# First adaLN pair in two channel halves, splits two units ahead and late loads in sixteen slots, before a 32-expert MoE

## The chip, the cores and the metric

The kernel runs on one NeuronCore of one Trainium2 chip. The metric is the device time of one execution in microseconds. TensorE is PE in the rows, VectorE DVE, ScalarE ACT, GpSimd POOL and SyncE SP; the queue of an engine that issues DMAs has a q behind its name (SPq).

## The reference, cut to what matters

256 tokens of width 1024 go through one layer; everything is float32.

```python
ada = (silu(c) @ w_ada + b_ada)                       # w_ada 1024 x 6144
sh_m, sc_m, g_m, sh_f, sc_f, g_f = split(ada, 6)
h = rms_norm(x, norm_mix_g) * (1 + sc_m) + sh_m
proj = h @ w_in                                       # w_in 1024 x 4000
q_lat, kv_lat, k_pe, u, c_gate, b_gate, g_attn, g_conv = split(proj)
a_branch = attention(q_lat, kv_lat, k_pe; w_uq, w_ukv) @ w_up_attn
c_branch = (b_gate * causal_conv3(c_gate * u)) @ w_up_conv
x = x + g_m * ((sigmoid(g_attn) * a_branch + sigmoid(g_conv) * c_branch) @ w_o)
h = rms_norm(x, norm_ffn_g) * (1 + sc_f) + sh_f
# top-4 of 32 experts; expert e: gu = h @ w_gu[e] + b_gu[e]; y = swiglu(gu) @ w_down[e] + b_down[e]
x = x + g_f * moe(h);  out = rms_norm(x) * g_final
```

The weights of the mixer are some 48 MB, those of the experts (w_gu 1024 x 2048 and w_down 1024 x 1024 for each of 32) some 403 MB. All are read once.

## The kernel before

**Two stages.** The front (adaLN, projections, attention, convolution, gates, w_o, router) takes the first 244 us of the profile; then the 32 experts follow, each for up to 64 tokens gathered by one-hot matmuls. Every engine works through its own instructions in the order in which the code emits them; nothing is reordered, so an instruction that waits holds up all behind it on that engine. The DMA queue of SP is such an order too: nearly all loads go through it.

**Slots.** All weights pass through one SBUF pool. In the front it is 22 "narrow" slots of 8 KB for each partition, and the MoE stage sees the same memory as 11 "wide" slots of 16 KB, wide slot i being narrow slots 2i and 2i+1. `take` hands out the free slot that has been free longest, `give` returns one, and `pump` issues the next loads of the list `loads` while more than `spare` slots are free. In the front `spare` is 9. Once the list is empty, `take` prefers a slot whose neighbour in the wide pair is free.

**Projections.** Weights come in "units" of [128, 4, 416 or 512] or [128, 2, 1024] (1 MB), k = 0 to 25, in the order in which they are used. `split` (lines 342 to 349) turns a raw unit into a high part (ACT copy, L346) and a low part (DVE subtraction, L347); each product is three matmuls (L335 to L337, or L477 in `proj`): high by high, high by low, low by high. The table `LOOK` sets for each unit how many later units are split by then.

**adaLN.** The first pair (shift_m, scale_m) needs all rows of w_ada by 2048 columns: eight chunks of 1 MB, 128 rows of 8 KB each (L120), then 32 matmuls of 512 columns (L251). The sums are transposed to columns (L320) and give `sh_col` and `a_col` (L330 to L332); with these the normalised x, transposed on PE (L302), becomes the high part of h (ACT, L417), a float32 copy (DVE, L420) and the low part (DVE, L423). The second pair (gate_m, shift_f) is multiplied on PE, the third (scale_f, gate_f) is accumulated on DVE chunk by chunk (L446) and summed over partitions by `ada_sum` on PE (L453), between the two halves of the attention branch.

**The end of the front.** After gate 3: the halves of the attention output (ACT L689, POOL L690), the attention branch with w_up_attn in two parts k = 0 and 1, `merge_t(0)` (transposes L797), `wo_mm(0, ...)`, `merge_t(1)`, `wo_mm(1, ...)` and the router. `bias_load` (L855) loads b_gu into a narrow slot by four DMAs on SP's queue, just after the last w_o unit and just ahead of the first expert weights (L999). `bias_table` (L863) works on it later, on ACT and POOL.

**The experts.** Each needs four w_gu loads and two w_down loads of 2 MB; each fills a wide slot as soon as both its narrow slots, or the load before in that slot, are done with.

Of the kernel before, what the change touches and what calls it, by code (L numbers as in the profile page):

```python
# [16 lines left out]
P = 128  # L17
D = 1024
# [33 lines left out]
def ap_of(a, offset, dims):  # L52
    return bass.AP(tensor=a.tensor, offset=a.offset + offset, ap=dims)
# [3 lines left out]
def block_kernel(ctx, tc, x, c, positions, w_ada, b_ada, norm_mix_g, w_in, q_norm_g, w_uq, kv_norm_g,  # L57
# [16 lines left out]
    class Slots:  # L74
        def __init__(self, pool, since, size):
            self.pool, self.since, self.held, self.clock, self.spare = pool, since, {}, max(since), 0

            for i in range(len(since)):
                pool.tile([P, size], F32, name="w", tag=f"w{i}", bufs=1)

        def take(self, shape, dtype=F32):

            i = min((not loads and self.since[(i ^ 1) % len(self.since)] is not None, c, i)
                    for i, c in enumerate(self.since) if c is not None)[2]
            self.since[i] = None
# [25 lines left out]
    def mmt():  # L111
        return mm.tile([P, 512], F32, name="mm")
# [4 lines left out]

    def ada0_chunk(j):
        w = slot([2048])
        load(w, ap_of(w_ada, j * 6 * D, [[8 * 6 * D, P], [1, 2048]]))  # L120
        return w
# [72 lines left out]
    with tc.tile_pool(name="front", bufs=1) as fr, \  # L194
# [29 lines left out]
        def rows_in(dst, src):  # L224
            return lambda: load(dst, src)
# [5 lines left out]
                 rows_in(pvec[18:19], kv_norm_g),  # L231
                 rows_in(pvec[19:31], conv_w.rearrange("o k (q p) -> (o k q) p", p=P))]
        small += [rows_in(brow[g][32 * b:32 * b + 1, :], b_ada[:, (4 * g + b) * 512:(4 * g + b + 1) * 512])
                  for g in range(3) for b in range(4)]
        ada0 = []
        for j in range(8):
            ada0.append(ada0_chunk(j))
            if j:
                for f in small[3 * j - 3:3 * j]:
                    f()  # L240

# [11 lines left out]

        def ada0_mm(j):
            ada_mm(pa, j, ada0[j])
            give(ada0[j])

# [9 lines left out]
        V.tensor_scalar(xn[:, 1, :], xs[:, 1, :], r0[:, 1:2], None, op0=ALU.mult)  # L267
        for j in range(2):
            ada0_mm(j)
        pos_f = ft("pos_f", [NT, P], 2, "pe1")  # L270
# [22 lines left out]

        for j in range(2, 6):
            ada0_mm(j)
        xps = []
        for q2 in range(4):
            p = (mmt() if q2 == 3 else tpt()).rearrange("p (q t) -> p q t", t=T)
            xps.append(p)
            for q in range(2):  # L300
                for i in range(NT):
                    TE.transpose(p[:, q, i * P:(i + 1) * P],  # L302
                                 xn[:, i, (2 * q2 + q) * P:(2 * q2 + q + 1) * P], ident)
        give(xn)
        for j in range(6, 8):
            ada0_mm(j)
        ppc = mmt()
# [18 lines left out]
        arow = slot([512])  # L326
        V.tensor_add(arow, brow[0], pa)
        pcv = halves_t(arow, mmt(), lambda q: slice(q * P, (q + 1) * P))
        give(arow)
        V.tensor_copy(by_half(sh_col[:, 0, :]), pcv[:, 0:2, :, 0])  # L330
        V.tensor_scalar(by_half(a_col[:, 0, :]), pcv[:, 2:4, :, 0], 1.0, None, op0=ALU.add)
        V.tensor_mul(a_col[:, 0, :], a_col[:, 0, :], gmix)  # L332

# [8 lines left out]

        def split(raw, shape):
            hi = slot(shape, F32R)
            lo = slot(shape, F32R)
            S.activation(hi, raw, AF.Copy)  # L346
            V.tensor_tensor(lo, raw, hi, op=ALU.subtract)  # L347
            give(raw)
            return [hi, lo]
# [6 lines left out]

        jobs = [win_unit(0, 416, h) for h in range(2)]
        jobs += [win_unit(928, 512, h) for h in range(2)]
        jobs += [([2, 768], w_uq.rearrange("o (q p) f -> p (o q) f", p=P)),
# [27 lines left out]
        units, chunks = [raw_load(*j) for j in jobs], [ada_load(*j) for j in ada_todo]  # L387
        loads += [(chunks if c == "a" else units).pop(0) for c in "wwwwwwwwwaaawwawwwwaaaawwwaawaawwwawawaaww"]
        narrow.spare = 9

        def ahead(n):
            while len(done) < min(n, len(jobs)):
                need(lambda: len(raws) > len(done))
                done.append(split(*raws[len(done)]))


        LOOK = [2, 2, 4, 3, 4, 1, 2, 0, 2, 0, 4, 1, 1, 0, 2, 2, 2, 1, 3, 3, 3, 0, 0, 0, 0, 0]

# [10 lines left out]


        ahead(1)
        hT = [slot([NQ, T], F32R), slot([NQ, T], F32R)]
        h32 = slot([NQ, T])
        for half in range(2):
# [9 lines left out]
            ahead(half + 2)  # L424
        give(h32)
        S.dma_start(rw.rearrange("p (a b) e -> p a b e", b=2), router_w.rearrange("o (a p b) e -> p (o a) b e", p=P, b=2))
# [55 lines left out]

        def projT(u, ps, half):
            for m in range(4):
                for q in range(4):
# [11 lines left out]

        pl = two()
        u = unit()
        proj(u, pl, 0, 416)  # L500
        proj(unit(), pl, 1, 416)
# [24 lines left out]

        pc_ = twoT()
        projT(unit(), pc_, 0)
        projT(unit(), pc_, 1)

# [856 lines left out]
```

## Time and profile before

| | |
|---|---|
| median of three runs | 1178.86 us (1177.23 to 1180.64) |
| the profiled execution, its own time | 1177.89 us |
| its span | 1176.2 us |
| mean granted clock of TensorE | 0.971 of full |
| PE busy | 1073.2 us, 91% |
| DVE, ACT, POOL busy | 360.1, 152.0 and 36.7 us |
| read from HBM | 455.79 MB, 388 GB/s over the span |

The page cuts the span into 40 slices of 29.4 us. Its line "DMA" gives the busy share of the 16 DMA engines in tenths, "GB/s" what they moved. A busy PE is not PE at its peak. The DMA line has to be read by stage: the mean over the span hides that the first eight slices are uneven and the rest are flat. The window view gives the same for any stretch, with the granted clock (PEclk). The wait view says for each line how long an engine or queue stood, and on whom. The timeline gives start and duration; what is in square brackets is the idle time just before, and what ended it.

### The profile page before, as it was taken

Reading aid. Unit: us, or ns where it says so; the run is one execution under the profiler, and the core shown is the slowest. Engines: PE = TensorE matmul, PEld = TensorE weight load, DVE = VectorE, ACT = ScalarE, POOL = GpSimd, SP = SyncE. Lnnn points to the kernel's source line nnn. Section 1 sums busy time; section 2 is a strip of 40 time slices with the busy share of each in tenths; the row PEclk is TensorE's granted clock in tenths of the full one; section 3 lists DMA queues with packets and bytes.
Section 4 is the critical chain, followed back from the end, with each engine's and each line's share of the span. In section 5 each row is a group of like instructions: output and inputs, shape, how many; then the busy total and the mean of one; then the engine's idle time right before and its main releaser. Section 6 shows DMA issues by size and latency. Waiting matters only on the chain. (4 is left out here: it accounts for less than half of the span.)

```text
span 1176.2 us, 11805 instructions
## 1 busy us (share of the span) xinstructions
PE 1073.2 (91%) x4914; PEld 492.1 (42%) x4914; DVE 360.1 (31%) x703; ACT 152.0 (13%) x261; POOL 36.7 (3%) x85
## 2 busy tenths in 40 slices
PE   5898997999999999999999879999888988898996
PEld 1887775753343343323433234334223422342333
DVE  3857588423221222111212112131212121211123
ACT  1545642211000010000000000000000000000001
POOL 1000003100000000000000000000000000000000
PEclk9899998979999999998999989999999999998998
DMA  9983853899999999999999999999999999999995
GB/s 362 354 286 116 316 210 146 359 428 428 428 428 428 428 426 417 427 429 427 428 427 428 427 426 428 427 427 427 428 427 427 428 427 427 427 428 428 427 420 180
DMA packets 48206, 457.66 MB, mean 389 GB/s; under 512 B 4939, under 2 KB 10088, under 8 KB 20756
## 3 DMA queue, kind: packets, MB, share of 16 engines
q1 hardware_dynamic: 47394, 456.58, 93.1%
q8 instruction: 41, 0.67, 0.2%
q10 hardware_dynamic: 674, 0.14, 0.1%
q0 software_dynamic: 80, 0.14, 0.0%
q14 instruction: 17, 0.14, 0.0%
HBM read 455.79 MB, written 1.05 MB: 388 GB/s over the span
## 5 line engine op out<-in xcount | busy, mean ns | idle before, releaser
L1072 PE MATMUL pg<-w,hsel 128*64 128x512 f32 x2048 | 458.6, 601 | 28.1 <-DMA w<-in_w_gu 28.0
L1072 PEld LDWEIGHTS pg<-w,hsel 128*64 128x64 f32 x2048 | 142.9, 138 | 328.1 <-issue 273.8
L1110 PE MATMUL pm<-w,aT 128*64 128x512 f32 (+1 forms) x1056 | 227.8, 582 | 12.1 <-DMA w<-in_w_down 10.5
L1090 DVE TENSOR_SCALAR ga<-pg 128x512 f32<-128x512 f32 x32 | 22.1, 691 | 463.3 <-PE pg L1072 447.1
L1110 PEld LDWEIGHTS pm<-w,aT 128*64 128x64 f32 x1056 | 74.3, 137 | 160.8 <-issue 133.3
L1091 ACT ACTIVATE sgm<-ga 128x512 f32<-128x512 f32 x32 | 20.2, 630 | 689.4 <-DVE ga L1090 689.4
L1116 DVE TENSOR_TENSOR yp<-gfx,pm 64x512 f32<-64x512 f32 x62 | 42.5, 685 | 199.9 <-PE pm L1110 199.4
L1044 PE MATMUL pm<-oh,xs 128*128 128x256 f32 (+1 forms) x256 | 58.6, 389 | 5.0 <-DVE oh L1031 5.0
L477 PE MATMUL mm<-w 128*128 128x512 f32 (+1 forms) x240 | 58.5, 404 | 3.0 <-ACT w L417 3.0
L347 DVE TENSOR_TENSOR w<-w 128x2048 fp32r<-128x2048 f32 (+3 forms) x26 | 57.2, 2235 | 8.3 <-ACT w L346 8.1
L1044 PEld LDWEIGHTS pm<-oh,xs 128*128 128x128 f32 x256 | 50.5, 204 | 16.6 <-issue 11.5
L335 PE MATMUL mm<-w 128*128 128x256 f32 (+1 forms) x160 | 54.9, 343 | 1.7 <-ACT w L689 1.2
L1135 PE MATMUL mm<-yp,s 128*128 128x512 f32 x120 | 54.9, 600 | 0.8 <-DVE yp L1116 0.8
L337 PE MATMUL mm<-w 128*128 128x256 f32 (+1 forms) x160 | 53.5, 334 | 2.1 <-POOL w L690 2.0
L336 PE MATMUL mm<-w 128*128 128x256 f32 (+1 forms) x160 | 53.2, 332 | 0.0
L477 PEld LDWEIGHTS mm<-w 128*128 128x128 f32 x240 | 47.8, 200 | 11.8 <-ACT w L417 3.9
L346 ACT ACTIVATE w<-w 128x2048 fp32r<-128x2048 f32 (+3 forms) x26 | 46.3, 1838 | 11.9 <-DMA w<-in_w_in 11.9
L335 PEld LDWEIGHTS mm<-w 128*128 128x128 f32 x160 | 31.0, 194 | 8.9 <-issue 3.9
L1135 PEld LDWEIGHTS mm<-yp,s 128*128 128x128 f32 x120 | 22.1, 190 | 29.9 <-issue 27.5
L1221 POOL CAST sel<-id 128x256 fp32r<-128x256 f32 x32 | 12.7, 402 | 684.0 <-PE pg L1224 683.9
L337 PEld LDWEIGHTS mm<-w 128*128 128x128 f32 x160 | 31.1, 194 | 6.2 <-POOL w L690 2.4
L251 PE MATMUL pa<-w,cact 128*32 128x512 f32 x128 | 22.1, 775 | 12.5 <-DVE rs_v L142 8.4
(282 smaller groups left out, 626.5 us busy)
## 6 DMA issues: line engine op xcount, KB each, us to landing
w<-in_w_gu SPq DMA_DIRECT2D x128, 2048.0 KB, 39.1
w<-in_w_down SPq DMA_DIRECT2D x62, 2048.0 KB, 39.1
w<-in_w_ada SPq DMA_DIRECT2D x24, 1024.0 KB, 5.8
w<-in_w_in SPq DMA_DIRECT2D x14, 1024.0 KB, 9.4
w<-in_w_o SPq DMA_DIRECT2D x4, 1024.0 KB, 7.0
w<-in_w_up_conv SPq DMA_DIRECT2D x2, 1024.0 KB
w<-in_w_up_attn SPq DMA_DIRECT2D x2, 1024.0 KB, 7.2
w<-in_w_down SPq DMA_DIRECT2D x4, 512.0 KB, 32.3
```

What stands on the lines that cost most here:

```text
L251: TE.matmul(pa[32 * b:32 * b + 32, :], cact[:, j:j + 1].to_broadcast([P, 32]), w[:, b * 512:(b + 1) * 512], start=(j == 0), stop=(j == 7), ...
L335: TE.matmul(o, l[0], r[0], start=start, stop=False, skip_group_check=True)
L336: TE.matmul(o, l[0], r[1], start=False, stop=False, skip_group_check=True)
L337: TE.matmul(o, l[1], r[0], start=False, stop=stop, skip_group_check=True)
L346: S.activation(hi, raw, AF.Copy)
L347: V.tensor_tensor(lo, raw, hi, op=ALU.subtract)
L477: TE.matmul(ps[i][:, :n], hT[l][:, 4 * half + q, i * P:(i + 1) * P], u[r][:, q, :], start=(half == 0 and q == 0 and l == 0 and r == 0), st ...
L1044: TE.matmul(p[:, q, :], xs[:, i, fcols(2 * q2 + q)], oh[:, i, :n], start=(i == 0), stop=(i == NT - 1))
L1072: TE.matmul(pg[64 * g:64 * g + 64, n, :], hs[k // 4][:, k % 4, c0:c0 + CAP], w[:, f0:f0 + 512], start=False, stop=(k == NQ - 1), skip_grou ...
L1110: TE.matmul(py[64 * h:64 * h + 64, :], aT[:, qa, 64 * g:64 * g + 64], w[:, h], start=(b == 0), stop=(b == 7), skip_group_check=True)
L1116: V.tensor_mul(yp[64 * k2:64 * k2 + 64, h * 512:(h + 1) * 512], gfx[hp, :], py[hp, :])
L1135: TE.matmul(acc[i][h], s2[:n, i * P:(i + 1) * P], yp[:n, h * 512:(h + 1) * 512], start=start, stop=False, skip_group_check=True)
```

## The change

1. **adaLN's first pair in two channel halves.** The 2048 columns are loaded as two halves of 512 shift and 512 scale columns. A chunk is now [128, 2, 2, 512], loaded by two DMAs of 512 KB with rows of 2 KB: four chunks for channels 0 to 511, four for channels 512 to 1023. The matmuls have 256 columns, 64 instead of 32. Each half has its own sum, transposes and columns (`cols0`) and its own `h_half`. The transposes of x come before them; the last two PSUM tiles are copied to SBUF (`xT1`). The first four units change order: both 416- and 512-column units of half 0, then those of half 1, and the loads are put between the chunks to match. `projT` of unit 1 has the last two chunks of half 1 between its column blocks.
2. **Low parts behind h.** For the first units the DVE subtraction of a split is kept back until `h_half` has been emitted.
3. **Splits and slots.** `LOOK` is nearly everywhere 2; `loads` alternates units and adaLN chunks; `spare` starts at 8 and falls to 4; from unit 10 on `take` uses only the first sixteen slots as long as one of them is free.
4. **b_gu** is loaded by POOL's queue.

```diff
@@ class Slots
+            self.upto = len(since)
         def take(self, shape, dtype=F32):
-
-            i = min((not loads and self.since[(i ^ 1) % len(self.since)] is not None, c, i)
-                    for i, c in enumerate(self.since) if c is not None)[2]
+            i = min((i >= self.upto, c, i) for i, c in enumerate(self.since) if c is not None)[2]
@@ adaLN
-    def ada0_chunk(j):
-        w = slot([2048])
-        load(w, ap_of(w_ada, j * 6 * D, [[8 * 6 * D, P], [1, 2048]]))
+    def ada0_chunk(hb, j2):
+
+        w = slot([2, 2, 512])
+        for k in range(2):
+            load(w[:, k], ap_of(w_ada, (2 * j2 + k) * 6 * D + 512 * hb, [[8 * 6 * D, P], [D, 2], [1, 512]]))
         return w
...
+        def cols0(hb, p):
+
+            cs = slice(256 * hb, 256 * hb + 256)
+            V.tensor_add(arow[:, cs], brow[0][:, cs], pa[:, cs])
+            for q in range(2):
+                TE.transpose(p[:, q * P:(q + 1) * P], arow[:, 256 * hb + q * P:256 * hb + (q + 1) * P], ident)
...
-        def split(raw, shape):
+        def split(raw, shape, later=None):
             hi = slot(shape, F32R)
             lo = slot(shape, F32R)
+
+            def low():
+                V.tensor_tensor(lo, raw, hi, op=ALU.subtract)
+                give(raw)
+
             S.activation(hi, raw, AF.Copy)
-            V.tensor_tensor(lo, raw, hi, op=ALU.subtract)
-            give(raw)
+            if later is None:
+                low()
+            else:
+                later.append(low)
             return [hi, lo]
...
-        jobs = [win_unit(0, 416, h) for h in range(2)]
-        jobs += [win_unit(928, 512, h) for h in range(2)]
+        jobs = [win_unit(c0, n, h) for h in range(2) for c0, n in ((0, 416), (928, 512))]
...
-        LOOK = [2, 2, 4, 3, 4, 1, 2, 0, 2, 0, 4, 1, 1, 0, 2, 2, 2, 1, 3, 3, 3, 0, 0, 0, 0, 0]
+        LOOK = [2, 1, 2, 3, 2, 2, 2, 2, 2, 2, 2, 2, 2, 2, 2, 2, 2, 2, 2, 2, 2, 0, 0, 0, 0, 0]
 
         def unit():
             k = taken[0]
             taken[0] += 1
+            narrow.spare = {4: 7, 8: 6, 14: 5, 18: 4}.get(k, narrow.spare)
+            if k == 10:
+                narrow.upto = 16
...
         pl = two()
-        u = unit()
-        proj(u, pl, 0, 416)
+        pc_ = twoT()
+        proj(unit(), pl, 0, 416)
+        ada0_mm(1, 0)
+        ada0_mm(1, 1)
+        projT(unit(), pc_, 0, (lambda: None, lambda: ada0_mm(1, 2), lambda: ada0_mm(1, 3), lambda: cols0(1, tpt())))
+        h_half(1)
+        lows.pop()()
+        give(arow, xT1, h32)
         proj(unit(), pl, 1, 416)
...
-                    load(raw[64 * k:64 * k + 64, t, :], rows[64 * t:64 * t + 64, :])
+                    G.dma_start(raw[64 * k:64 * k + 64, t, :], rows[64 * t:64 * t + 64, :])
```

How the order of instructions moves. **SP's queue at the end of the front**, before (w is a slot, xN a run of N equal rows):

```order
L375 DMA w<-in_w_ada 128x2048 x2
L382 DMA w<-in_w_o 128x2x1024 x2
L855 DMA w<-in_b_gu 64x512 x4
L999 DMA w<-in_w_gu 128x4096 x8
L999 DMA w<-in_w_down 128x4096 x2
```

and after:

```order
L402 DMA w<-in_w_o 128x2x1024
L395 DMA w<-in_w_ada 128x2048 x2
L402 DMA w<-in_w_o 128x2x1024 x3
L1048 DMA w<-in_w_gu 128x4096 x8
L1048 DMA w<-in_w_down 128x4096 x2
```

The four loads of b_gu are gone from between w_o and w_gu. They stand in **POOL's queue** now, behind the scaled router weights (rwa) and ahead of the bias table (bg):

```order
L739 TENSOR_TENSOR w<-w 128x512 x2
L977 TENSOR_SCALAR rwa<-rw,a_col 128x32 x8
L904 DMA w<-in_b_gu 64x512 x4
L912 TENSOR_TENSOR bg_1955<-w,bg_1955 64x1024
L915 CAST id_94<-ident 64x64 x2
```

Nothing else on POOL changes place. **DVE in the first adaLN pair**, before (L327 is the sum with b_ada, L347 a low part of a unit, L420 and L423 the two steps of h, L142 the start of the latents' root):

```order
L327 TENSOR_TENSOR w<-brow,pa 128x512
L330 COPY sh_col<-mm 128x8
L331 TENSOR_SCALAR a_col<-mm 128x8
L332 TENSOR_TENSOR a_col<-a_col,pcol 128x8
L347 TENSOR_TENSOR w<-w 128x1664
L420 TENSOR_SCALAR w<-tp,a_col,sh_col 128x256 x4
L423 TENSOR_TENSOR w<-w 128x1024
L347 TENSOR_TENSOR w<-w 128x1664
```

and after (L339 is the sum, L362 a low part, L454 and L457 the steps of h), the second half:

```order
L339 TENSOR_TENSOR w<-brow,pa 128x256
L344 COPY sh_col<-tp 128x4
L345 SCALAR_TENSOR_TENSOR a_col<-tp,pcol 128x4
L454 TENSOR_SCALAR w<-w,a_col,sh_col 128x256 x4
L457 TENSOR_TENSOR w<-w 128x1024
L362 TENSOR_TENSOR w<-w 128x1664
L362 TENSOR_TENSOR w<-w 128x2048
L362 TENSOR_TENSOR w<-w 128x1536
```

The low parts moved behind h, and the sum and the columns exist once for each half.

## Rows read from the trace of the kernel before

**Rows 1.** The page: DMA busy tenths and GB/s in 40 slices.

```profile
DMA  9983853899999999999999999999999999999995
GB/s 362 354 286 116 316 210 146 359 428 428 428 428 428 428 426 417 427 429 427 428 427 428 427 426 428 427 427 427 428 427 427 428 427 427 427 428 428 427 420 180
```

**Rows 2.** The page: chain that ended last, by engine.

```profile
DMA 30%; PE 10%; DVE 0%; issue 0%; ACT 0%; DVEq 0%; SPq 0%; ACTq 0%
```

**Rows 3.** Windows: stretch, length, busy us by engine, PEclk, DMA share, GB/s.

```profile
187.50:207.00 19.50, 16.42 (x76) 12.11 (x76) 14.64 (x17) 4.90 (x5) 6.39 (x8) 0.91 0.01 2
207.00:244.00 37.00, 33.13 (x169) 27.30 (x168) 17.18 (x56) 11.04 (x23) 3.97 (x6) 0.88 0.95 388
244.00:700.00 456.00, 431.89 (x1866) 163.68 (x1866) 101.38 (x210) 24.29 (x44) 7.20 (x18) 0.98 1.01 427
```

**Rows 4.** Waits of SP's queue, 150 to 300 us: total us, times, longest.

```profile
SPq L855 <- DVE w L729: 20.2, 1, 20.2
SPq L999 <- PE mm L337: 16.5, 2, 13.1
...
SPq L855 <- PE tp L797: 7.1, 1, 7.1
```

**Rows 5.** Timeline of SP's queue, 178 to 275 us: start us, us, line.

```profile
179.04 0.89 SPq L382 DMA_DIRECT2D w<-in_w_o  x2
207.22 2.48 SPq L855 DMA_DIRECT2D w<-in_b_gu  x4
209.75 20.27 SPq L999 DMA_DIRECT2D w<-in_w_gu  x8
```

**Rows 6.** Timeline of PE: last matmuls of attention branch, wo_mm(1,1,4,6), wo_mm(1,1,6,8).

```profile
198.23 0.40 PE L337 MATMUL mm<-w 128*128 128x512 f32 x1
...
225.70 0.39 PE L337 MATMUL mm<-w 128*128 128x512 f32 x1
...
229.26 0.40 PE L337 MATMUL mm<-w 128*128 128x512 f32 x1
```

**Rows 7.** Line L999, all expert loads: time from issue to landing.

```profile
DMA to landing us min/median/max: 20.9/39.1/41.1
```

**Rows 8.** DMA view, 8 to 28 us, then 34 to 48 us.

```profile
DMA packets 1423, 7.77 MB, mean 389 GB/s; under 512 B 153, under 2 KB 540, under 8 KB 552
...
DMA packets 2894, 5.36 MB, mean 383 GB/s; under 512 B 611, under 2 KB 611, under 8 KB 2891
```

**Rows 9.** Timeline of PE: first projection; first matmul of unit 6.

```profile
32.84 0.91 PE L477 MATMUL mm<-w 128*128 128x416 f32 x2 [1.18 <-ACT w L417]
35.56 11.21 PE L477 MATMUL mm<-w 128*128 128x416 f32 x46 [1.81 <-ACT w L417]
...
58.69 0.37 PE L335 MATMUL mm<-w 128*128 128x256 f32 x1
```

**Rows 10.** Timeline of DVE, 26 to 60 us.

```profile
33.86 1.90 DVE L420 TENSOR_SCALAR w<-tp,a_col,sh_col 128x256 f32<-128x256 f32 x4
36.00 1.22 DVE L423 TENSOR_TENSOR w<-w 128x1024 fp32r<-128x1024 f32 x1 [0.24 <-ACT w L417]
...
43.23 6.16 DVE L347 TENSOR_TENSOR w<-w 128x2048 fp32r<-128x2048 f32 x3 [0.58 <-ACT w L346]
49.31 0.16 DVE L142 TENSOR_SCALAR rs_v<-ls 128x4 f32<-128x4 f32 x1
...
54.46 3.60 DVE L347 TENSOR_TENSOR w<-w 128x1024 fp32r<-128x1024 f32 x2
```

**Rows 11.** Timeline of PE: its waits in the attention branch.

```profile
177.46 0.50 PE L335 MATMUL mm<-w 128*128 128x512 f32 x1 [1.21 <-ACT w L689]
...
180.19 0.63 PE L337 MATMUL mm<-w 128*128 128x512 f32 x1 [2.00 <-POOL w L690]
...
190.27 1.62 PE L453 MATMUL pa<-w,ones 128*32 128x512 f32 x8 [3.20 <-DVE w L446]
```

**Rows 12.** Windows behind the last two of these waits.

```profile
180.20:187.00 6.80, 6.80 (x22) 5.21 (x22) 6.80 (x3) 0.00 (x0) 3.22 (x1) 0.75 0.98 370
...
191.90:198.60 6.70, 6.70 (x26) 5.46 (x27) 4.65 (x7) 0.00 (x0) 0.00 (x0) 0.84 0.00 0
```

More of the change, by code (lines that the diff above doesn't have):

```diff
@@ L232, in block_kernel @@
                  rows_in(pvec[19:31], conv_w.rearrange("o k (q p) -> (o k q) p", p=P))]
+        small += [rows_in(brow[0][32 * b:32 * b + 1, :].rearrange("o (h c) -> o h c", h=2),
+                          ap_of(b_ada, b // 2 * D + b % 2 * 256, [[1, 1], [512, 2], [1, 256]])) for b in range(4)]
         small += [rows_in(brow[g][32 * b:32 * b + 1, :], b_ada[:, (4 * g + b) * 512:(4 * g + b + 1) * 512])
[L234 to L240, printed above, removed]
+                  for g in range(1, 3) for b in range(4)]
+        ada0 = {}
+        for j2 in range(3):
+            ada0[0, j2] = ada0_chunk(0, j2)
+            for f in small[5 * j2:5 * j2 + 5]:
+                f()
         cact = keep.tile([P, 8], F32, name="cact")
@@ L252, in ada_mm, with ada0_mm @@
                           w[:, b * 512:(b + 1) * 512], start=(j == 0), stop=(j == 7), skip_group_check=True)
-        def ada0_mm(j):
-            ada_mm(pa, j, ada0[j])
-            give(ada0[j])
+        def ada0_mm(hb, j2):
+            w = ada0.pop((hb, j2))
+            for k in range(2):
+                j = 2 * j2 + k
+                for b in range(4):
+                    TE.matmul(pa[32 * b:32 * b + 32, 256 * hb:256 * hb + 256], cact[:, j:j + 1].to_broadcast([P, 32]),
+                              w[:, k, b // 2, b % 2 * 256:b % 2 * 256 + 256], start=(j == 0), stop=(j == 7),
+                              skip_group_check=True)
+            give(w)
         ss = keep.tile([P, NT], F32, name="ss")
@@ L267, in block_kernel @@
         V.tensor_scalar(xn[:, 1, :], xs[:, 1, :], r0[:, 1:2], None, op0=ALU.mult)
-        for j in range(2):
-            ada0_mm(j)
+        xps = []
+        for q2 in range(4):
+            p = (mmt() if q2 == 3 else tpt()).rearrange("p (q t) -> p q t", t=T)
+            xps.append(p)
+            for q in range(2):
+                for i in range(NT):
+                    TE.transpose(p[:, q, i * P:(i + 1) * P],
+                                 xn[:, i, (2 * q2 + q) * P:(2 * q2 + q + 1) * P], ident)
+        give(xn)
+        xT1 = slot([2, 2, T])
+        S.activation(xT1[:, 0], xps[2], AF.Copy)
+        V.tensor_copy(xT1[:, 1], xps[3])
+        xps[2:] = [xT1[:, 0], xT1[:, 1]]
         pos_f = ft("pos_f", [NT, P], 2, "pe1")
@@ L292, in block_kernel @@
             S.activation(dst, dst, AF.Sin)
[L294 to L306, printed above, removed]
         ppc = mmt()
@@ L326, in block_kernel @@
         arow = slot([512])
[L327 to L332, printed above, removed]
+        def cols0(hb, p):
+            cs = slice(256 * hb, 256 * hb + 256)
+            V.tensor_add(arow[:, cs], brow[0][:, cs], pa[:, cs])
+            for q in range(2):
+                TE.transpose(p[:, q * P:(q + 1) * P], arow[:, 256 * hb + q * P:256 * hb + (q + 1) * P], ident)
+            pcv = p[:, :2 * P].rearrange("p (q v b r) -> p v b q r", q=2, v=2, b=2)[:, :, :, :, 0]
+            ks = slice(4 * hb, 4 * hb + 4)
+            V.tensor_copy(sh_col[:, 0, ks].rearrange("p (b q) -> p b q", q=2), pcv[:, 0])
+            V.scalar_tensor_tensor(a_col[:, 0, ks].rearrange("p (b q) -> p b q", q=2), pcv[:, 1], 1.0,
+                                   gmix[:, ks].rearrange("p (b q) -> p b q", q=2), op0=ALU.add, op1=ALU.mult)
         def mul3(o, l, r, start, stop):
@@ L387, in block_kernel, with ahead @@
         units, chunks = [raw_load(*j) for j in jobs], [ada_load(*j) for j in ada_todo]
-        loads += [(chunks if c == "a" else units).pop(0) for c in "wwwwwwwwwaaawwawwwwaaaawwwaawaawwwawawaaww"]
-        narrow.spare = 9
-        def ahead(n):
+        loads += [(chunks if c == "a" else units).pop(0) for c in "wwwwwwwwwaawawawwawawawawwaawawawawawaawww"]
+        narrow.spare = 8
+        def ahead(n, later=None):
             while len(done) < min(n, len(jobs)):
                 need(lambda: len(raws) > len(done))
-                done.append(split(*raws[len(done)]))
-        LOOK = [2, 2, 4, 3, 4, 1, 2, 0, 2, 0, 4, 1, 1, 0, 2, 2, 2, 1, 3, 3, 3, 0, 0, 0, 0, 0]
+                done.append(split(*raws[len(done)], later))
+        LOOK = [2, 1, 2, 3, 2, 2, 2, 2, 2, 2, 2, 2, 2, 2, 2, 2, 2, 2, 2, 2, 2, 0, 0, 0, 0, 0]
         def unit():
@@ L407, in drop, with h_half @@
             give(*u)
-        ahead(1)
+        need(lambda: raws)
+        ada0[0, 3] = ada0_chunk(0, 3)
+        for f in small[15:]:
+            f()
+        need(lambda: len(raws) > 1)
+        for j2 in range(2):
+            ada0[1, j2] = ada0_chunk(1, j2)
+        need(lambda: len(raws) > 2)
+        for j2 in range(2, 4):
+            ada0[1, j2] = ada0_chunk(1, j2)
         hT = [slot([NQ, T], F32R), slot([NQ, T], F32R)]
         h32 = slot([NQ, T])
-        for half in range(2):
+        def h_half(half):
             for k in range(4):
@@ L423, in block_kernel @@
             V.tensor_sub(hT[1][:, hs_, :], h32[:, hs_, :], hT[0][:, hs_, :])
-            ahead(half + 2)
-        give(h32)
+        for j2 in range(3):
+            ada0_mm(0, j2)
+        lows = []
+        ahead(1, lows)
+        ada0_mm(0, 3)
+        cols0(0, mmt())
+        h_half(0)
+        lows.pop()()
+        ahead(2)
+        ahead(3, lows)
         S.dma_start(rw.rearrange("p (a b) e -> p a b e", b=2), router_w.rearrange("o (a p b) e -> p (o a) b e", p=P, b=2))
@@ L480, in proj, with projT @@
             drop(u)
-        def projT(u, ps, half):
+        def projT(u, ps, half, between=()):
             for m in range(4):
+                for f in between[m:m + 1]:
+                    f()
                 for q in range(4):
@@ L498, in block_kernel @@
         pl = two()
-        u = unit()
-        proj(u, pl, 0, 416)
+        pc_ = twoT()
[4 more added lines that the diff above has]
+        h_half(1)
+        lows.pop()()
+        give(arow, xT1, h32)
         proj(unit(), pl, 1, 416)
@@ L525, in block_kernel @@
             V.tensor_copy(kk[:, i, :, DN:], kr[:, i].to_broadcast([P, H, DR]))
-        pc_ = twoT()
-        projT(unit(), pc_, 0)
         projT(unit(), pc_, 1)
```

## The prediction

> **What bounds the kernel now.** I read the page's DMA line first, then the chain of waits, then windows by stage, then the queue of SP at the seam between them. The page shows two kernels in one: eight uneven slices, and from the ninth slice on 426 to 429 GB/s in nearly every one, up to the last [rows 1]. The chain that ended last is made of DMA far more than of PE [rows 2]. From 244 to 700 us the DMA engines are fully busy at 427 GB/s while PE is busy 431.89 of 456 us [rows 3]. So the expert stage runs at the speed of its loads: a load of 2.097 MB takes 2.097 / 0.427 = 4.9 us, and no expert load is quicker from issue to landing than 20.9 us [rows 7], so that about 20.9 - 4.9 = 16 us of other loads are still ahead of the best placed one. PE can therefore not be sped up usefully there, and the end of the kernel is the start of the load stream plus a fixed sum of bytes. **The start is what counts.** From 187.5 to 207 us the DMA engines move 2 GB/s [rows 3]: nothing. SP issued its last w_o loads at 179.04 and 0.89 us later stood before b_gu until 207.22, 20.2 us for a DVE result (L729) and 7.1 us more for PE's transposes of merge_t(1) (L797) [rows 4, 5]. Behind it in the same queue stand all expert loads, the first of which goes out at 209.75 [rows 5].
>
> **The change part by part.**
>
> *b_gu by POOL, and the slots kept free (edits 3 and 4).* These belong together. With b_gu out of SP's queue the first expert load waits only for its own slot, and the cap of sixteen slots leaves three wide slots (six narrow ones) out of use late in the front. Following the new order of slots through the code, with times of before as a ruler: loads 0 and 1 need the end of the attention branch, PE at 198.23 + 0.40 = 198.6; loads 2 and 3 need the split of w_o and merge_t(1), below 207.3; load 4 the end of wo_mm(1,1,0,4), about 213.5, ahead of the row at 225.70; load 5 the end of wo_mm(1,1,4,6), 225.70 + 0.39 = 226.1; loads 6 and 7 the end of wo_mm(1,1,6,8), 229.26 + 0.40 = 229.7 [rows 6]. A stream that is never hungry later is as early as its worst load allows, so I take from each release the loads ahead of it: load 0 198.6; load 5 226.1 - 5 x 4.9 = 201.6; load 6 229.7 - 6 x 4.9 = 200.3. The worst is load 5, 201.6: the first five loads are done about 223 to 225 us and the engines idle 2 or 3 us for the sixth. Before, load 0 binds at 209.75 (SP's longest wait behind it, 13.1 us on PE's L337 [rows 4], falls under five loads already queued). Gain: 209.75 - 201.6 = **8.2 us**, if PE's clock time in the front stays where it was. Later the stream keeps its reserve: some 16 us of queue [rows 7] against 8.2 us by which it now runs ahead.
>
> The cost of b_gu on POOL: it stands behind rwa, which ends near 207, and in front of the bias table only. The price of a DMA issue by POOL for such a load is not in the trace; SP's four take 2.48 us [rows 5], and the DMA work of 0.5 MB is 1.2 us at 427 GB/s, in either queue. The bias table is not needed until more than 20 us later. I take nothing for it, up to 2.5 us as its upper end, nothing as its lower, as the cover is there.
>
> A rule of the Trainium skill speaks against this edit: the page "DMA: Bandwidth & Descriptors", section "Rules for kernel authors", says that spreading DMAs over issuing engines brings no bandwidth, since all run on the same 16 DMA engines, and saves only issue time. By that rule alone the edit is worth SP's issue time and no more. The trace does not contradict it, but shows another thing at stake: SP's place in line, not bandwidth.
>
> *adaLN in halves (edits 1 and 2).* Rows of 2 KB instead of 8 KB: in 8 to 28 us, mostly 8 KB rows, the engines ran at 389 GB/s, and in 34 to 48 us, where nearly all packets are under 8 KB, at 383 [rows 8]. On 8.4 MB that is 0.3 us; I allow up to 2. What is gained first: half 0 is complete after x, four chunks and a unit, 6.1 instead of 9.4 MB, about 8.5 us sooner at 389 GB/s, so the first projection comes near 24 instead of 32.84 [rows 9]. But half 1 now comes behind three units as well, 12.2 MB, 31 to 33 us of transfer behind a start of 2 to 3 us: 34 to 36 us. PE then needs the last chunks' matmuls and some of unit 1; I put the sum of half 1 between 36.5 and 42 us. From there DVE has a chain in order: sum and columns with PE's transposes, about 1.2; four steps of h 1.90; its low part 1.22 with a short wait 0.24; the low parts of units 2, 3 and w_uq, 6.16 less 0.4 for the narrower unit, 5.8; the latents' root, scaling and ropes from 49.31 to 54.46, 5.15; the low parts of w_ukv and unit 6, 3.60 [rows 10]. Sum 19.1 us, so unit 6's third matmul can start between 55.6 and 61.1, against 58.69 + 0.3 = 59.0 [rows 9]. PE's work up to there is the same in sum and is done before that. So the front arrives at unit 6 between 3.4 us earlier and 2.1 us later: what half 0 gained in time is spent as an earlier idle. I take **0**.
>
> *Splits two ahead and the new load order (edit 3).* From unit 6 to gate 3 PE is nearly gapless, so looking ahead cannot gain much; it can only lose where a load comes late, and the loads that I followed are issued some 15 to 30 us before their unit. In the attention branch PE waits 1.21 us (ACT's half), 2.00 (POOL's half) and 3.20 (DVE's adaLN sums for ada_sum) [rows 11], and after the last two the clock is low for a while: mean 0.75 over 6.80 us and 0.84 over 6.70 us, that is 1.7 and 1.1 us lost [rows 12]. The DVE order before ada_sum holds one low part less than before, worth between 0 and 3.2 us; the other two waits are untouched in the order. I take 0, from the row of the untouched two, and keep -3 as an end.
>
> **Sum.** 1177.89 (the profiled time; its span of 1176.2 and 1.7 around it) - 8.2 + 0 + 0 = 1169.7. The median of the runs is 1.0 above the profiled one, so 1170 is what I give.
>
> **The rivals.**
>
> *The front gets shorter too.* If the three waits of the attention branch go, 1.2 + 2.0 + 3.2 us, with the low clock behind them, 2.8 us, the stream starts 9.2 us earlier still: 1169.7 - 9.2 = 1160.5. For: DVE is idle near 30 to 40 us and has less queued late. Against: ACT's and POOL's halves depend on the last attention product, whose place does not change.
>
> *The start hardly moves.* Either the front comes later by 5 to 8 us, through a unit that lands late under the tighter slots, and eats the gain: 1175 to 1178. Or only the issue time goes, as when the queue's place was not what held the stream: 1177.89 - 2.5 = 1175.4. For: sixteen slots and a queue in order make every late release a late load. Against: SP's wait of 27.3 us on one item, with idle DMA engines behind [rows 3, 4]. The rule of the skill named above would give this time; I give it 3 of the 15 in 100.
>
> *Slower: half 1 of adaLN holds everything.* All later stages stand behind h's second half. If its last chunk lands late, because half-size DMAs with 2 KB rows go slower than [rows 8] say, the whole front moves and the stream with it. It decides from 8.2 + 3.5 = 11.7 us of delay at unit 6; this needs the sum of half 1 at 51.6 us or later, ten us behind my latest. At 14 us the time is 1183.7.
>
> **How the numbers follow.** Forecast 65 in 100 (1167 to 1173 by the ends above), a shorter front 13, hardly moved 15, slower 7. A difference of 0.3%, 3.5 us, is about what can be told from no change. Faster: 65 + 13 = 78; same 15; slower 7. The range leaves out the slower case and the outer ends of the two others: 1160 to 1177.
>
> **What would show it.** In the changed trace: first w_gu issue near 199 instead of 209.75; five loads quickly, the sixth near 226, a short dip of the DMA rate just before; then a flat 427 GB/s to an end 8 us earlier; unit 6 of PE near 59; the three waits of the attention branch still there. It is wrong if unit 6 starts after 65, if SP stands on another item between 180 and 199, or if a slice after the ninth falls under 410 GB/s, which would say that the stream ran into slots that PE had not yet released.

## The result and the profile after

The changed kernel takes 1169.55 us (median of 4 runs, 1167.3 to 1170.66); the kernel before took 1179.32 in the same comparison (1177.23 to 1180.64). The ratio is 0.9916, 95% interval 0.9894 to 0.9938: 0.8% faster, forecast 1170. The profiled execution is the slowest of the four, 1170.66 with a span of 1169.0, so its span is 7.2 us below that of before; the medians are 9.8 us apart.

The page after, its span and its DMA lines (to be read beside [rows 1]):

```profile
span 1169.0 us, 11947 instructions
DMA  8974584999999999999999999999999999999995
GB/s 312 390 277 145 219 349 155 396 427 429 427 428 427 427 427 418 428 427 426 429 428 427 427 428 426 427 427 428 428 427 427 427 427 429 427 426 428 429 420 184
```

From the ninth slice on hardly anything has changed: 426 to 429 GB/s, the same dip in the middle (417 before, 418 now), nearly the same two slices at the end. The experts still run at the speed of their loads. What moved is where this flat part begins, and that is seen in windows and in SP's queue. The same windows as [rows 3], then SP's queue as in [rows 5], then the longest waits of that queue as in [rows 4]:

```profile
187.50:207.00 19.50, 16.42 (x73) 12.17 (x72) 16.94 (x18) 4.69 (x4) 5.49 (x7) 0.91 0.33 122
207.00:244.00 37.00, 33.43 (x176) 27.48 (x174) 17.05 (x51) 11.34 (x23) 7.26 (x11) 0.90 1.01 402
```

```profile
174.57 2.63 SPq L402 DMA_DIRECT2D w<-in_w_o  x3
199.64 31.89 SPq L1048 DMA_DIRECT2D w<-in_w_gu  x8
231.63 0.90 SPq L1048 DMA_DIRECT2D w<-in_w_down  x2
```

```profile
SPq L1048 <- PE pg L1121: 51.0, 10, 15.0
SPq L1048 <- PE mm L351: 29.6, 3, 20.6
SPq L1048 <- PE tp L933: 12.6, 1, 12.6
```

The stretch in which the engines moved 2 GB/s now moves 122, and from 207 us on they are busy throughout. The first expert load goes out at 199.64 instead of 209.75. SP's wait on b_gu is gone; in its place SP waits for PE itself, 20.6 us at most, for the end of the attention branch (the 51.0 us on L1121 are later loads that wait for the experts). The 12.6 us are load 5, which goes out at 227.07. The view puts this wait down to the router's first product (L933), which overlaps the end of wo_mm(1,1,4,6); the last matmul of wo_mm(1,1,4,6) ends at 226.65 + 0.39 = 227.04:

```profile
226.65 0.39 PE L351 MATMUL mm<-w 128*128 128x512 f32 x1
```

What the front does now (PE from the first projection to unit 6; DVE in the chain behind the second half's sum; PE's waits in the attention branch, as in [rows 9], [rows 10] and [rows 11]):

```profile
26.22 7.36 PE L520 MATMUL mm<-w 128*128 128x416 f32 x24 [0.92 <-ACT w L451]
...
57.84 0.39 PE L349 MATMUL mm<-w 128*128 128x256 f32 x1 [1.11 <-ACT w L365]
60.46 0.58 PE L351 MATMUL mm<-w 128*128 128x256 f32 x1 [2.11 <-DVE w L362]
```

```profile
40.76 0.42 DVE L339 TENSOR_TENSOR w<-brow,pa 128x256 f32<-128x256 f32 x1 [7.77 <-PE pa L262]
...
46.15 5.76 DVE L362 TENSOR_TENSOR w<-w 128x1664 fp32r<-128x1664 f32 x3
...
56.98 3.42 DVE L362 TENSOR_TENSOR w<-w 128x1024 fp32r<-128x1024 f32 x2
```

```profile
181.87 0.50 PE L349 MATMUL mm<-w 128*128 128x512 f32 x1 [1.21 <-ACT w L738]
183.23 0.50 PE L351 MATMUL mm<-w 128*128 128x512 f32 x1 [0.64 <-POOL w L739]
191.29 1.07 PE L496 MATMUL pa<-w,ones 128*32 128x512 f32 x8 [2.77 <-DVE w L489]
```

The first projection starts 6.6 us sooner, the third matmul of unit 6 all the same 1.5 us later (60.46 against 59.0), because DVE's chain from 40.76 to 60.40 ends last; DVE stood idle 7.77 us just ahead of that chain. At ada_sum the front is 1.0 us behind that of before (191.29 against 190.27).

### The profile page after: what moved, and what is told of

Its sections match the earlier page's. It is cut to its first block, busy times and chain, and to the rows that moved or that the text cites. A ratio compares the mean times of both kernels' runs of the same rounds, so it can differ in the third digit from the quotient of the medians.

```text
span 1169.0 us, 11947 instructions
## 1 busy us (share of the span) xinstructions
PE 1071.6 (92%) x4978; PEld 495.4 (42%) x4978; DVE 359.3 (31%) x706; ACT 153.3 (13%) x262; POOL 37.0 (3%) x89
## 5 line engine op out<-in xcount | busy, mean ns | idle before, releaser
L1121 PE MATMUL pg<-w,hsel 128*64 128x512 f32 x2048 | 458.1, 601 | 27.0 <-DMA w<-in_w_gu 26.8
L1121 PEld LDWEIGHTS pg<-w,hsel 128*64 128x64 f32 x2048 | 143.0, 138 | 326.4 <-issue 275.6
L1140 ACT ACTIVATE sgm<-ga 128x512 f32<-128x512 f32 x32 | 20.2, 630 | 687.3 <-DVE ga L1139 687.3
L362 DVE TENSOR_TENSOR w<-w 128x2048 fp32r<-128x2048 f32 (+3 forms) x26 | 56.7, 2201 | 13.9 <-ACT w L365 13.8
L349 PE MATMUL mm<-w 128*128 128x256 f32 (+1 forms) x160 | 55.9, 350 | 2.8 <-ACT w L738 1.2
L351 PE MATMUL mm<-w 128*128 128x256 f32 (+1 forms) x160 | 54.5, 340 | 3.0 <-DVE w L362 2.3
L350 PE MATMUL mm<-w 128*128 128x256 f32 (+1 forms) x160 | 53.9, 337 | 0.0
L1150 PE MATMUL pm<-ident,sgm 128*128 128x128 f32 x128 | 23.8, 309 | 10.4 <-ACT s L1113 7.9
```

The lines of the kernel that those rows point to most:

```text
L349: TE.matmul(o, l[0], r[0], start=start, stop=False, skip_group_check=True)
L350: TE.matmul(o, l[0], r[1], start=False, stop=False, skip_group_check=True)
L351: TE.matmul(o, l[1], r[0], start=False, stop=stop, skip_group_check=True)
L1121: TE.matmul(pg[64 * g:64 * g + 64, n, :], hs[k // 4][:, k % 4, c0:c0 + CAP], w[:, f0:f0 + 512], start=False, stop=(k == NQ - 1), skip_grou ...
L1150: TE.transpose(p[:, q, :], a[:, q::4], ident)
```

## The experiments

**One law for all runs.** For every kernel below I read from its trace when its sixteenth expert load (load 15) landed, by the bytes that had come in; this is good to about 0.5 us, and single DMA engines end up to 2.6 us later. In the last column is the span less this time.

| kernel | first w_gu issue | load 15 landed | span | span - landing |
|---|---|---|---|---|
| before | 209.75 | 290.5 | 1176.2 | 885.7 |
| changed | 199.64 | 283.7 | 1169.0 | 885.3 |
| bgu_only | 179.60 | 278.0 | 1163.8 | 885.8 |
| bgu_back | 197.76 | 281.1 | 1166.6 | 885.5 |
| no_cap | 206.97 | 290.3 | 1175.5 | 885.2 |
| adaln_only | 213.86 | 294.7 | 1180.3 | 885.6 |
| late_only | 195.04 | 283.5 | 1168.7 | 885.2 |
| adaln_bgu | 193.91 | 282.3 | 1167.8 | 885.5 |
| full_slots | 176.84 | 278.5 | 1164.6 | 886.1 |
| small_late | 197.59 | 281.9 | 1167.9 | 886.0 |
| low2_early | 196.16 | 280.6 | 1165.8 | 885.2 |
| mix | 170.53 | 274.5 | 1160.6 | 886.1 |

Over 20 us of difference in the front the rest is the same to 0.9 us. So the end is set by where the load stream stands once it no longer waits for the front. The first issue alone doesn't tell this: bgu_only issues its first load 20 us before the changed kernel and ends 5.2 us earlier, because loads 6 and 11 to 15 still wait for PE.

**bgu_only.** The kernel before with one line changed.

```diff
-                    load(raw[64 * k:64 * k + 64, t, :], rows[64 * t:64 * t + 64, :])
+                    G.dma_start(raw[64 * k:64 * k + 64, t, :], rows[64 * t:64 * t + 64, :])
```

> The kernel before with one line changed: b_gu is loaded by POOL's queue; slots, splits and adaLN are those of before. Theory A (the end is set by the start of the expert stream, and each expert load goes out as soon as its slot is free): in the old order of slots loads 0 to 4 wait for work that ends between 176 and 199 us (gate 3, the adaLN sums, the attention branch), load 5 for wo_mm(1,0) and (1,1) near 206, load 6 for wo_mm(1,1,4,6) at 225.9, so the sixth load is no longer the worst one; the worst are load 6 (225.9 - 6 x 4.9 = 196.5) and loads 11 to 15, released by PE at 250.5 to 270.7 (250.5 - 11 x 4.9 = 196.6, 270.7 - 15 x 4.9 = 197.2). Gain 209.75 - 197 = 12 to 13 us: 1165 to 1167, which is less than the whole change has. Theory B (as the prediction put it, queue and capped slots belong together, and without the cap the loads come free late): gain at most 3 us, 1175 to 1178. Theory C (the front became shorter, the queue is nothing): 1178.

1166.34 us against 1177.36, ratio 0.9917 (0.9899 to 0.9935): by the ratio as much as the whole change. (The kernel before had medians of 1177.2 to 1179.3 in the comparisons of this document, so differences of 2 us between two changed versions are not settled by their times alone.) SP's queue:

```profile
178.62 0.89 SPq L382 DMA_DIRECT2D w<-in_w_o  x2
179.60 49.94 SPq L999 DMA_DIRECT2D w<-in_w_gu  x8
```

Not a microsecond lies between the last w_o load and the first expert load. Theory A holds, B and C fall: with the slots of before, the queue alone is enough.

**bgu_back.** The changed kernel with the line above undone.

```diff
-                    G.dma_start(raw[64 * k:64 * k + 64, t, :], rows[64 * t:64 * t + 64, :])
+                    load(raw[64 * k:64 * k + 64, t, :], rows[64 * t:64 * t + 64, :])
```

> The changed kernel with b_gu back on SP's queue, ahead of the expert loads. Theory A: in the new order of slots b_gu gets a slot that the adaLN sums free near 193 us, before the first expert load can go (199.6), so it holds nobody up: 1169 to 1171 as the changed kernel, first w_gu issue at 199.6 to 200. Theory B (b_gu's place in SP's queue is what cost the 8 us, by itself): back at 1177 to 1179, first w_gu near 210.

1168.49 us, ratio to before 0.9931 (0.9914 to 0.9948), no worse than the changed kernel's 0.9916.

```profile
172.70 2.63 SPq L402 DMA_DIRECT2D w<-in_w_o  x3
190.56 2.46 SPq L904 DMA_DIRECT2D w<-in_b_gu  x4
197.76 31.73 SPq L1048 DMA_DIRECT2D w<-in_w_gu  x8
```

b_gu stands ahead of the expert loads again and holds nobody up: its slot is free at 190.56, the first expert's only at 197.76. In the full change the move to POOL's queue is worth nothing.

**no_cap.** The changed kernel without the cap.

```diff
-                narrow.upto = 16
+                narrow.upto = 22
```

> The changed kernel without the cap: all 22 narrow slots may be used to the end of the front; b_gu stays on POOL's queue. Theory A: load 0 then waits for the low part of the last w_o unit (near 206), load 1 for wo_mm(1,1,0,2) near 213, and the stream is as late as load 1 allows, 213 - 4.9 = 208: only 1 to 2 us ahead of before, 1175.5 to 1177.5. Theory B (the queue alone brings the gain, the cap nothing): 1169 to 1171.

1176.8 us against 1177.36, ratio 0.9996 (0.9987 to 1.0006): the gain is gone.

```profile
166.80 4.41 SPq L402 DMA_DIRECT2D w<-in_w_o  x3
206.97 22.70 SPq L1048 DMA_DIRECT2D w<-in_w_gu  x8
```

With the new load order the late units lie across all slots, so that no wide slot is free before 206.97. The slots of before had left wide slots free from 180 us on, behind b_gu. So the cap makes good what edit 3 itself takes away. Whether that is its order of loads is not shown: edit 3 also drops the old rule of `take` that prefers a slot whose neighbour is free once the list is empty, and no run takes the one without the other.

**adaln_only.** The halves and the late low parts alone; load order, `LOOK` from the fifth unit on, `spare`, slot rule and b_gu's queue as before. Against the changed kernel:

```diff
-        loads += [(chunks if c == "a" else units).pop(0) for c in "wwwwwwwwwaawawawwawawawawwaawawawawawaawww"]
+        loads += [(chunks if c == "a" else units).pop(0) for c in "wwwwwwwwwaaawwawwwwaaaawwwaawaawwwawawaaww"]
...
-        LOOK = [2, 1, 2, 3, 2, 2, 2, 2, 2, 2, 2, 2, 2, 2, 2, 2, 2, 2, 2, 2, 2, 0, 0, 0, 0, 0]
+        LOOK = [2, 1, 2, 3, 4, 1, 2, 0, 2, 0, 4, 1, 1, 0, 2, 2, 2, 1, 3, 3, 3, 0, 0, 0, 0, 0]
...
-                    G.dma_start(raw[64 * k:64 * k + 64, t, :], rows[64 * t:64 * t + 64, :])
+                    load(raw[64 * k:64 * k + 64, t, :], rows[64 * t:64 * t + 64, :])
```

> The adaLN halves and the low parts behind h alone: load order, splits from the fifth unit on, spare, slots and b_gu's queue are those of before. Theory A: b_gu waits on SP's queue for the low part of the last w_o unit, near 207 to 208, the first expert load goes out near 210: no gain, 1178 to 1180, and PE reaches unit 6 near 60.5 as in the changed kernel (58.9 before). Theory C (the halves shorten the front and this is the gain): 1169 to 1173.

1180.54 us against 1177.36, ratio 1.0025 (1.0013 to 1.0036): slower, just beyond the expected 1178 to 1180.

```profile
211.30 2.46 SPq L902 DMA_DIRECT2D w<-in_b_gu  x4
213.86 20.16 SPq L1046 DMA_DIRECT2D w<-in_w_gu  x8
```

b_gu blocks as before, 4 us later, because the whole front is later. Theory C falls: the halves carry none of the gain.

**late_only.** The complement: adaLN in one piece, all of edits 3 and 4 (but of `LOOK`, the first four entries of before stay except the third, and `spare` starts at 9).

```diff
-        LOOK = [2, 2, 4, 3, 4, 1, 2, 0, 2, 0, 4, 1, 1, 0, 2, 2, 2, 1, 3, 3, 3, 0, 0, 0, 0, 0]
+        LOOK = [2, 2, 2, 3, 2, 2, 2, 2, 2, 2, 2, 2, 2, 2, 2, 2, 2, 2, 2, 2, 2, 0, 0, 0, 0, 0]
...
+            if k == 10:
+                narrow.upto = 16
```

> The late parts of the change alone: new load order, splits two ahead (the first four units as before), spare, cap of sixteen and b_gu on POOL's queue, with the adaLN of before in one piece. Theory A: the slots fall otherwise than in the full change, so that load 4, not load 5, waits for wo_mm(1,1,4,6): 225.9 - 4 x 4.9 = 206.3, worth 3.4 us; besides the late front is about 2.9 us shorter (in the changed kernel gate 4 starts 3.9 us later than before and ada_sum only 1.0 later), together 6 us: 1170 to 1172.5 where before is 1177.4. Rival (the adaLN halves carry the gain): 1176 to 1178.

1170.44 us against 1177.23, ratio 0.9946 (0.9927 to 0.9965). Both parts of the expectation show in the trace: load 4 goes out at 222.47, after wo_mm(1,1,4,6), and is the worst one; and ada_sum is 3.6 us earlier than before ([rows 11]):

```profile
186.70 1.25 PE L456 MATMUL pa<-w,ones 128*32 128x512 f32 x8 [2.77 <-DVE w L449]
```

**adaln_bgu.** adaln_only with b_gu on POOL's queue.

```diff
-                    load(raw[64 * k:64 * k + 64, t, :], rows[64 * t:64 * t + 64, :])
+                    G.dma_start(raw[64 * k:64 * k + 64, t, :], rows[64 * t:64 * t + 64, :])
```

> The adaLN halves with load order, splits and slots of before and b_gu on POOL's queue (the run of the halves alone plus that one line). Theory A: the stream is released by PE again, loads 7 and 11 to 15, and PE's front is later by the 4 us that the halves cost when alone (first experts at 255.0 instead of 250.5): 1166.3 + 4 = 1169 to 1171. Rival (the halves cost nothing once the queue is free): 1165 to 1167.

1168.48 us against 1177.23, ratio 0.9924 (0.9908 to 0.9941), between the two expectations. The profiled span is 4.0 us longer than that of bgu_only, the median only 2.1, and the intervals of the two ratios overlap. That the halves cost something is shown by adaln_only, not here.

**full_slots.** The changed kernel with another slot rule.

```diff
-            i = min((i >= self.upto, c, i) for i, c in enumerate(self.since) if c is not None)[2]
+            i = min((i >= self.upto, not loads and self.since[(i ^ 1) % len(self.since)] is not None, c, i)
+                    for i, c in enumerate(self.since) if c is not None)[3]
...
-                narrow.upto = 16
+                narrow.upto = 18
```

> The changed kernel with the slot rule of the mixed version: cap of eighteen from unit 10 on, and within it a slot whose neighbour in the wide pair is free goes first; the adaLN halves stay. Theory A: load 5 no longer waits for wo_mm(1,1,4,6), which falls to load 7 (227 - 7 x 4.9 = 192.7); the stream is released by PE in loads 11 to 15 (272 - 15 x 4.9 = 198.5, some 3 us before the changed kernel): 1164.5 to 1167, and the 3 to 4 us that separate it from the mixed version (1163.0) are the price of the adaLN halves. Rival (load 5 was not what bound the changed kernel): 1169 to 1170.

1166.59 us against 1178.10, ratio 0.9902 (0.9885 to 0.992). Load 5 goes out at 207.72 and the wait for wo_mm(1,1,4,6) falls to load 7:

```profile
176.84 50.08 SPq L1049 DMA_DIRECT2D w<-in_w_gu  x8
```

The time lies in Theory A's range and not in the rival's, but by the ratios, 0.9902 against 0.9916, the two versions are not told apart. Loads 0 to 4 go out earlier here too, so this run doesn't show that load 5 alone bound the changed kernel.

**small_late.** In the changed kernel the DMA engines run nearly dry at 11 to 14 us, while SP issues small loads of b_ada ahead of the third chunk. I moved those behind the chunks.

```diff
-            for f in small[5 * j2:5 * j2 + 5]:
+            for f in (small[0:5], small[5:6], small[6:10])[j2]:
                 f()
...
+        for f in small[10:]:
+            f()
```

> The changed kernel with its small bias loads moved on SP's queue: the four pieces of brow[0] behind the third chunk, the eight pieces of the other pairs behind the last chunk. Theory D (the DMA engines run dry at 11 to 14 us because SP issues nine small loads ahead of the third chunk, and everything behind is late by that): the sum of half 1 comes 2 to 2.5 us earlier, unit 6 starts at 58 to 59 instead of 60.5, the time falls by 1.5 to 2.5 us to 1167 to 1168. Rival (PE's and DVE's own chain sets unit 6): unit 6 stays at 60 to 60.5 and the time at 1169 to 1170.

1169.24 us against 1177.23, ratio 0.9932 (0.9914 to 0.995): no difference from the changed kernel. The DMA rate in 40 slices of 0 to 62 us, the changed kernel and then this one:

```profile
GB/s 0 111 420 399 402 368 287 61 98 377 374 386 363 350 377 394 402 387 384 378 383 384 389 385 377 358 370 406 400 378 388 387 386 420 422 423 390 395 420 375
```

```profile
GB/s 0 100 415 399 402 380 284 292 368 214 326 363 393 388 396 391 389 394 371 383 384 389 373 161 36 3 55 272 398 416 416 383 389 392 381 398 439 424 423 369
```

The hole moved from 11 us to 37 us, where eight small loads now stand ahead of the next units; the sum of half 1 came 1.0 us earlier and unit 6's third matmul 1.0 later. Theory D is refuted as I built it. Whether small loads that go through another queue would help was not tried.

**low2_early.** The low part of unit 2 ahead of the sum of half 1.

```diff
-        ahead(3, lows)
+        ahead(3)
...
         h_half(1)
-        lows.pop()()
```

> The changed kernel with one low part put back ahead of h: that of unit 2 (416 columns, second half) is emitted before the sum of half 1 instead of behind h. Theory E (unit 6 is late by DVE's chain behind the sum of half 1, 40.8 to 60.3 us in the changed kernel, while DVE stands idle for 7.8 us just ahead of it): the 1.9 us of this low part move into the idle time, unit 6's third matmul starts at 58.5 to 59 instead of 60.5, and everything behind is 1 to 2 us earlier: 1167.5 to 1169 where the changed kernel has 1169.5, gate 4 at 104.5 to 106 instead of 106.6. Rival (the time is set by PE's own work there, or what is gained is lost again to its clock): gate 4 unchanged within 0.5 us, 1169 to 1170.

The mechanism shows: the third matmul of unit 6 starts at 58.19, and gate 4 at 103.5, earlier than expected.

```profile
58.19 0.39 PE L351 MATMUL mm<-w 128*128 128x256 f32 x1 [2.11 <-DVE w L362]
```

The time doesn't tell: 1168.2 us against 1178.1, ratio 0.992 (0.9905 to 0.9935), where the changed kernel had 0.9916. Inconclusive within 0.2%.

**mix.** adaLN in one piece, b_gu on POOL's queue, new load order, splits and `spare`, the slot rule of full_slots. Against late_only:

```diff
-            i = min((i >= self.upto, c, i) for i, c in enumerate(self.since) if c is not None)[2]
+            i = min((i >= self.upto, not loads and self.since[(i ^ 1) % len(self.since)] is not None, c, i)
+                    for i, c in enumerate(self.since) if c is not None)[3]
...
-        LOOK = [2, 2, 2, 3, 2, 2, 2, 2, 2, 2, 2, 2, 2, 2, 2, 2, 2, 2, 2, 2, 2, 0, 0, 0, 0, 0]
+        LOOK = [2, 2, 4, 3, 4, 2, 2, 2, 2, 2, 2, 2, 2, 2, 2, 2, 2, 2, 2, 2, 2, 0, 0, 0, 0, 0]
...
-                narrow.upto = 16
+                narrow.upto = 18
```

> A version meant to beat both: the adaLN of before in one piece, b_gu on POOL's queue, the new load order, splits two ahead and falling spare, with a cap of eighteen slots from unit 10 on that also prefers a slot whose neighbour in the wide pair is free. Theory A: loads 0 and 1 go out near 178, load 5 near 213, load 6 near 215, load 7 near 226, so that the stream waits for PE in the first experts alone; with b_gu's line alone 12 us were gained; the later loads allow 2 to 2.6 us more and the late front 2.9 us: 1160 to 1163 where before is 1177.4. Rival (the first experts' PE time is all that is left, and the late front does not get shorter without the halves): 1165 to 1167.

1162.97 us against 1177.23, ratio 0.988 (0.9863 to 0.9896): faster than both kernels.

```profile
170.53 52.46 SPq L1003 DMA_DIRECT2D w<-in_w_gu  x8
```

```profile
GB/s 360 366 258 214 218 343 379 314 365 409 430 427 427 429 425 419 429 427 429 426 428 427 427 426 427 427 428 427 429 427 428 427 427 429 427 428 426 429 411 175
```

Slices 6 to 10 show what is left: expert loads already move from 170 us on, and now the stream waits for PE here and there until some 270 us, when load 15 goes out. Beside full_slots (0.9902), which has the halves and also the first entries of `LOOK` and the first value of `spare` that go with them, it is 0.2% faster, 2.6 us, and 4.0 us between the two profiled spans; the intervals just overlap.

## Why the prediction was right, point by point

**What bounds: right.** The law above is the prediction's first part: the end is the start of the stream plus a fixed sum of bytes. It held in twelve traces. One row under it was misread: [rows 7] covers only the loads of which the view tells a landing. Load 0 was in 7.4 us after its issue, at 217.2. For the reserve it makes no difference, as load 15 still took 20.2 us.

**Load 5: right in size, with luck.** Its own wait ended at 227.07, 1.0 us later than the ruler of before said (226.1), since the front is 1.0 us later. As a limit on the stream this is 227.07 - 5 x 4.9 = 202.6, 7.2 us ahead of 209.75, and 7.2 us is the difference of the two profiled spans. But load 5 did not hold the stream up in this trace. Loads 2 and 3 took 6.6 us each instead of 4.9, in the stretch in which POOL's b_gu loads ran; load 4 was in only near 230, and the engines were full when load 5 went out:

```profile
224.00:228.00 4.00, 3.85 (x24) 3.27 (x22) 2.54 (x9) 1.89 (x6) 0.00 (x0) 1.00 1.01 430
```

So the dip of the rate that I expected ahead of load 5 isn't there. What held was the start of load 0 and the time lost beside b_gu: 199.64 + 2 x (6.6 - 4.9) = 203.0, within 0.5 us of load 5's limit. That the two lie so close is luck. The term for b_gu on POOL, taken as 0 with 2.5 as its upper end, was 3.4 us, and it fell into the 2 or 3 us for which the engines were to wait for load 5.

Load 5 by itself is seen in bgu_back, where SP had loaded b_gu before: loads 2 and 3 take 4.9 us each, load 5 goes out at 225.12, and the queue does run nearly empty:

```profile
224.50:226.00 1.50, 1.41 (x11) 1.21 (x9) 1.29 (x8) 1.21 (x3) 0.00 (x0) 1.00 0.05 22
```

Its limit there is 225.12 - 5 x 4.9 = 200.6, 9.1 us ahead of 209.75; the span is 9.6 us shorter than that of before.

**"These belong together": wrong.** The step that put queue and slots into one term was never tested against the slots of before. There, loads 0 to 4 could go out between 179 and 199 us (bgu_only), so that the queue alone gives 12.4 us of span. In the full change, the cap gives the gain without the queue (bgu_back), and without the cap the queue gives nothing (no_cap). So the edit list has two keys to one door, and edit 3 is what locks it for the other key. The forecast was right because I followed the slots of the full change; had I been asked for the parts, I would have been off by some 9 us for the queue alone.

The rule of the Trainium skill ("DMA: Bandwidth & Descriptors", section "Rules for kernel authors") is that issuing engines share the same DMA engines, so that spreading saves only issue time. The trace agrees with it in bgu_back, where the queue is worth nothing (0.9931 there, 0.9916 with the queue). It says nothing of what bgu_only shows: one load that waited for its slot held five others behind it whose slots were free.

**adaLN in halves: inside its bounds, but not at their middle.** The sum of half 1 came at 40.76 (bounds 36.5 and 42), the chain behind it took 19.6 us (19.1 worked out), unit 6's third matmul started at 60.46 (55.6 to 61.1). What the term left out is what PE does while it waits. Windows of PE from 55 to 70 us, before and after:

```profile
55.00:70.00 15.00, 15.00 (x116) 12.93 (x114) 10.92 (x17) 7.59 (x12) 0.00 (x0) 1.00 0.53 166
```

```profile
55.00:70.00 15.00, 11.78 (x73) 10.36 (x73) 10.92 (x19) 8.45 (x10) 0.00 (x0) 0.77 0.53 202
```

PE had two waits, 3.2 us together, and its granted clock was 0.77 on average in place of 1.00. Gate 4 so starts 3.9 us later than before in the profiled run and 2.1 later in that of bgu_back, which has the same front; taken alone, the halves cost 0.25% (adaln_only).

**Splits and the late front: mis-sized the other way.** I took 0 with -3 as an end. Between gate 4 and ada_sum the changed kernel wins 2.9 us: POOL's wait is 0.64 instead of 2.00, that for the adaLN sums 2.77 instead of 3.20, and the clock from 176 to 200 us is 0.93 where the same window of before has 0.86. I had called POOL's half untouched; its place in the order is, but not its time. POOL's two subtractions took 2.54 us instead of 5.93. In before DVE worked all through them; in the changed kernel DVE stood idle, as its next low part was waiting for ACT. POOL and DVE, before and after:

```profile
177.49 5.93 POOL L690 TENSOR_TENSOR w<-w 128x512 fp32r<-128x512 f32 x2 [19.28 <-ACT w L689]
178.93 3.36 DVE L446 SCALAR_TENSOR_TENSOR w<-w,cact 128x2048 f32<-128x2048 f32 x1
```

```profile
181.90 2.54 POOL L739 TENSOR_TENSOR w<-w 128x512 fp32r<-128x512 f32 x2 [19.28 <-ACT w L738]
184.17 2.42 DVE L362 TENSOR_TENSOR w<-w 128x2048 fp32r<-128x2048 f32 x1 [2.89 <-ACT w L365]
```

late_only has the late parts without the halves and is 3.6 us earlier at ada_sum. The two errors, +3.9 and -2.9, nearly cancel. The 0 that I took for the front was right as a sum only.

**The rivals.** The shorter front came half true and was paid back by the halves. "The start hardly moves" is what no_cap is; "slower" is what adaln_only is, at 4 us of delay, not 14.

## What to carry to other kernels

Where a stage is bound by a stream of loads, find the load that is worst, release time less its place times the price of a load, price every edit by that load, and see in the trace whether the engines do run dry ahead of it; the first issue can move by 20 us for 5 us of time (changed kernel and bgu_only). A small load that waits for its slot in an in-order queue costs whatever stands ready behind it, so ask what is already free there before adding rules that keep things free. And test parts of a change singly: here one line is worth the whole, and the adaLN halves are a loss that the other edits hide.

## What the runs showed of the hardware

b_gu is four loads of 128 KB each. Issued by SP, the one whose landing the trace tells was in after 2.6 us, in before and in bgu_back. Issued by POOL in the changed kernel, they took 7.2 to 13.9 us, beside the expert loads:

```profile
DMA to landing us min/median/max: 7.2/10.6/13.9
```

From 205 to 224 us the DMA engines of the changed kernel were fully busy and yet moved 379 GB/s; in bgu_back they moved 425 in the same stretch. The changed kernel, then bgu_back:

```profile
205.00:224.00 19.00, 18.75 (x87) 14.04 (x86) 7.09 (x10) 3.26 (x8) 5.70 (x6) 1.00 1.01 379
```

```profile
205.00:224.00 19.00, 18.75 (x88) 14.13 (x87) 5.86 (x11) 3.71 (x9) 1.54 (x2) 1.00 1.00 425
```

So the stream lost 3.4 us to 0.5 MB that are worth 1.2 us at 427 GB/s. Load 5 could not go out before 227.07 anyway, so little was lost here. Two more versions with b_gu on POOL's queue moved 380 (small_late) and 373 GB/s (low2_early) in this stretch. Why it is slower was not tried.

POOL's subtraction of 128x512 (the low half of the attention output) took 1.28 to 1.30 us in the seven traces in which DVE stood idle for nearly all of that time. It took 2.58 to 3.34 us in the five in which DVE worked for most of it (before, bgu_only, adaln_only, adaln_bgu and mix), and DVE's adaLN step of 128x2048 beside it took 3.35 to 3.37 instead of 2.34. No run was made to test this alone.
